# Order of the high and low products of the channel blocks, and the place of their low parts, in an encoder block in split precision

## The chip, the cores and the metric

The program runs on one core of a Trainium2 chip. The metric is the device time of one execution in microseconds. Before the change it is 1772.78 us, the median of three runs (1772.76 to 1772.98).

## The reference

The reference is one layer of a bidirectional encoder on 256 tokens and 2048 channels, in float32:

```
proj = x @ w_in                          # q, k, v, r, af, ab, hy_u, gate_logits
y_gla = gla(q, k, v, r, af, ab, ...)     # chunked gated linear attention, both directions
y_hy  = hyena(hy_u, ...)                 # gated long convolutions
mix = (g0 * (y_gla @ w_gla_o) + g1 * (y_hy @ w_hy_o)) @ w_out
h = layernorm(alpha * x + mix)
out = layernorm(alpha * h + square(relu(h @ w_ff1)) @ w_ff2)
```

q and k have 1024 columns each, w_ff1 has 8192.

## The kernel before, in words

Every weight arrives in float32 and is split into a high part (rounded to the type that TensorE multiplies at full rate) and a low part (what is left). ScalarE casts the high part, VectorE subtracts it from the source to give the low part. Activations are split in the same way and lie as `act[:, kt, 0 or 1, tokens]`: for each of 16 row tiles `kt`, 256 columns of high parts and then 256 of low parts. Three products are wanted for each pair of tiles: high by high, high by low, low by high.

There are two kinds of weight blocks, of 128 x 2048 numbers each, split in halves of 1024 columns. In a *token block* (r, v, g, u, the output projections) the activation tile is loaded into TensorE and the weights stream, 512 columns at a time. In a *channel block* (the gate ranks, q, k, and f, the first matrix of the MLP) the weight tile of 128 columns is loaded and the activation streams. The high tile meets 512 columns at once (high and low activations, a *wide* product), the low tile only the 256 high columns (a *narrow* product). A channel block has 16 tiles, so 16 wide and 16 narrow products, all summed into one bank of PSUM; the two halves of the bank are added afterwards.

`channel_products` (L187) issues one half of a channel block, eight tiles. The first half issues its eight wide products (L193) and then its eight narrow ones (L197); the second half the eight narrow ones and then the eight wide ones. A block is so 8 wide, 16 narrow, 8 wide.

It is called from three places. `channel_pair` (L215) does the blocks of q and k that the opening of the kernel has not already done: 4 of q and 8 of k. `ff1_first` (L1340) does the first eight blocks of f. Three of these are begun earlier, token half by token half, and ended in `finish_block` (L233), which calls `channel_products` for the second half of the third one only; the other five are plain. `ff_pairs` (L1418) does the remaining 56 blocks of f, one in each of its `SLOTS` steps, between the products of the second MLP matrix (called w, L1378 to L1380: all 512 columns wide, 21 in a step, 15 ahead of the block and 6 behind it).

`weight_half` (L151) hands out the tiles of a half: a high tile from three buffers in turn and a low tile from three others in turn. A low buffer has 1032 columns. With `by_channel` the low part takes columns 0 to 1023, without it columns 8 to 1031:

```
return (wp.tile([P, D // 2], F32R, tag="whi", bufs=3, name=f"whi{n}_{h}"),
        lo[:, 0:D // 2] if by_channel else lo[:, 8:])
```

`fetch` (L112) loads a block and splits it by way of `weight_half` and `split_hi_lo` (L103), some blocks ahead of its use; blocks 0 to 16 (gate ranks, q, k) and 177 to 184 (the first eight of f) are by channel. In `ff_pairs` the same is done by `half_split` (L1331), by channel as well.

The order of the instructions on each engine comes from a planner with its own costs; within `ff_pairs` the casts and subtractions are kept in program order.

Of the kernel before, what the change touches and what calls it, by code (L numbers as in the profile page):

```python
# [20 lines left out]
KT = D // P  # L21
# [9 lines left out]
W_OUT_END = 177  # L31
LEAD = 8
FF_PAIRS = W_OUT_END + LEAD
# [16 lines left out]
def block_kernel(  # L50
# [26 lines left out]
    MM = nc.tensor.matmul  # L77
# [19 lines left out]
    def psum_main(name):  # L97
        return mmp.tile([P, 512], F32, tag="mm", name=name)
# [4 lines left out]
    def split_hi_lo(hi, lo, src):  # L103
        return (nc.scalar.copy(hi, src),  # L104
                nc.vector.tensor_tensor(lo, src, hi.bitcast(F32), op=ALU.subtract))  # L105
# [6 lines left out]
    def fetch():  # L112
        n = fetched[0]
        if n >= stop_at[0]:
            return
        fetched[0] = n + 1
        raw = wp.tile([P, D], F32, tag="raw", bufs=3, name=f"raw{n}")
        nc.sync.dma_start(raw, wblk[n])
        parts = []
        for h in range(2):  # L120
            hi, lo = weight_half(n, h, n < 17 or W_OUT_END <= n < FF_PAIRS)
            last_low[0] = split_hi_lo(hi, lo, raw[:, h * 1024:(h + 1) * 1024])[1]
            parts.append((hi, lo))
            if paced[0]:
                tc.keep_in_program_order(last_low[0])
                fill()
        queue.append(parts)
# [10 lines left out]
    def fill(every=False):  # L138
        tick[0] += 1
        budget[0] = min(budget[0], PACE / 2) + PACE  # L140
        while filling:
            e = min(filling, key=lambda e: e[:2])
            if not every and (e[0] > tick[0] or e[2] > budget[0]):
                break
            filling.remove(e)
            budget[0] -= e[2]
            e[3]()
# [3 lines left out]
    def weight_half(n, h, by_channel=False):  # L151
        i = low_turn[0] % 3
        low_turn[0] += 1
        lo = (base, wp, wp)[i].tile([P, D // 2 + 8], F32R, tag=f"wlo{i}", bufs=1, name=f"wlo{n}_{h}")
        return (wp.tile([P, D // 2], F32R, tag="whi", bufs=3, name=f"whi{n}_{h}"),
                lo[:, 0:D // 2] if by_channel else lo[:, 8:])
# [21 lines left out]
    def next_block():  # L178
        fetch()
        return queue.popleft()  # L180

    FULL = slice(0, L)
# [1 line left out]
    def channel_psum(name):  # L184
        return psum_main(name).rearrange("p (a b) -> p a b", a=2)

    def channel_products(ps, act, half, kts, ts=FULL, opens=True):  # L187
        hi, lo = half
        at = [(kt, slice(kt % 8 * P, (kt % 8 + 1) * P)) for kt in kts]

        def high():
            for kt, js in at:
                MM(ps[:, :, ts], hi[:, js], act[:, kt, :, ts], start=(kt == 0 and opens), stop=(kt == KT - 1))  # L193

        def low():
            for kt, js in at:
                MM(ps[:, 0, ts], lo[:, js], act[:, kt, 0, ts], start=False, stop=False)  # L197

        for part in (high, low) if kts[0] == 0 else (low, high):
            part()  # L200
# [14 lines left out]
    def channel_pair(act, name, dst, scale=1.0):  # L215
        for c in range(2):
            ps = channel_psum(f"{name}_{c}")
            parts = next_block()
            for h in range(2):
                channel_products(ps, act, parts[h], range(8 * h, 8 * h + 8))  # L220
            channel_sum(dst[:, c], ps, f"{name}_l{c}", scale)
            pump()

    def high_by_tokens(ps, act, half, kts, ts):
        for kt in kts:
            MM(ps[:, :, ts], half[0][:, kt % 8 * P:(kt % 8 + 1) * P], act[:, kt, :, ts],
               start=(kt == 0 and ts.start == 0), stop=False)

    def low_of_all(ps, act, half, kts):
        for kt in kts:  # L230
            MM(ps[:, 0], half[1][:, kt % 8 * P:(kt % 8 + 1) * P], act[:, kt, 0], start=False, stop=(kt == KT - 1))

    def finish_block(ps, act, parts, n):  # L233
        for h in range(n):
            high_by_tokens(ps, act, parts[h], range(8 * h, 8 * h + 8), slice(P, L))
        for h in range(n):
            low_of_all(ps, act, parts[h], range(8 * h, 8 * h + 8))
        for h in range(n, 2):
            channel_products(ps, act, parts[h], range(8 * h, 8 * h + 8))

    def token_half(pss, act, half, tbs, kt0, ends=(0, KT - 1), order=lambda ins: ins):
        hi, lo = half
# [54 lines left out]
    with tc.tile_pool(name="xp", bufs=1) as xp, tc.tile_pool(name="xq", bufs=1) as xq:  # L297
# [44 lines left out]
        for k0, n in PIECES:  # L342
            raw = pieces[k0]
            kts = range(k0, k0 + n)
# [11 lines left out]
            if k0 == 0:  # L356
                hi, lo = places[0]
# [162 lines left out]
    for i in range(2 * NCH):  # L520
        c, o = divmod(i, 2)
        n = 4 + (i * 21) // 15
# [16 lines left out]
    for _ in range(2):  # L539
        fetch()  # L540
# [487 lines left out]
    def resident_pieces(parts, order=lambda ins: ins):  # L1028
        for part in parts:
            n = fetched[0]  # L1030
            fetched[0] = n + 1
            raw = wp.tile([P, D], F32, tag="raw", bufs=3, name=f"raw{n}")
            nc.sync.dma_start(raw, wblk[n])
            for h, (hi, lo) in enumerate(part):
                order(split_hi_lo(hi, lo, raw[:, h * 1024:(h + 1) * 1024])[1])
        return parts

    def resident(slots):
        return resident_pieces([[(hi[:, c:c + 1024], lo[:, c:c + 1024]) for c in (0, 1024)] for hi, lo in slots])

    def halves(pool, tag, name):
        t = pool.tile([P, 4, D], F32R, tag=tag, name=name)
        return [(t[:, 0], t[:, 1]), (t[:, 2], t[:, 3])]
# [71 lines left out]
    parts = resident([x0] + halves(ep, "f", "wr1"))  # L1115
# [5 lines left out]
    for tb in range(NT):  # L1121
        column_products(pss, mT, parts, [tb], 1)
        if tb == 1:
            fetch()
# [113 lines left out]
    def cast(hi, src):  # L1238
        return pin(nc.scalar.copy(hi, src))  # L1239

    def rest(lo, src, hi):
        return VT(lo, src, hi.bitcast(F32), ALU.subtract)
# [81 lines left out]
    def block_load(p):  # L1324
        if block_raw[p % 2] is None:
            block_raw[p % 2] = ep.tile([P, D], F32, tag=("xl", "fraw")[p % 2], name=f"fraw{p}")
        nc.sync.dma_start(block_raw[p % 2], wblk[FF_PAIRS + 1 + 2 * p])
# [1 line left out]
    half_parts = {}  # L1329

    def half_split(p, h):  # L1331
        hi, lo = weight_half(FF_PAIRS + 1 + 2 * p, h, True)
        src = block_raw[p % 2][:, h * 1024:(h + 1) * 1024]
        cast(hi, src)
        rest(lo, src, hi)
        half_parts[p, h] = (hi, lo)
        if h and p + 2 < SLOTS:
            block_load(p + 2)

    def ff1_first():  # L1340
        begun = begin_three()
        for c2 in range(LEAD // 2):
            for c in range(2):
                if begun:
                    ps, parts, n = begun.pop(0)
                    finish_block(ps, hT, parts, n)
                else:
                    ps = channel_psum(f"f{c2}_{c}")
                    parts = next_block()
                    for h in range(2):  # L1350
                        channel_products(ps, hT, parts[h], range(8 * h, 8 * h + 8))
                summed = quad_sum(c2, c, ps, f"f{c2}_l{c}")
                at = 2 * c2 + c
                if at in (LEAD - 4, LEAD - 3):
                    block_load(at - LEAD + 4)
                if at in (LEAD - 3, LEAD - 2):
                    ring_load(at - LEAD + 3)
                if at == LEAD - 2:
                    plain_split(0)
                    pair_split(0)  # L1360
            squares(c2)
            forms(c2)
            for g in ((), (0,), (1, 2), (3,))[c2]:
                zc = z1[:, 1, g * 512:(g + 1) * 512]
                with tc.issue_after(summed.ins):
                    nc.vector.tensor_tensor(zc, zc, rows1[:, 1, g * 512:(g + 1) * 512], op=ALU.add)
# [51 lines left out]
    def ff_pairs():  # L1418
        pss = [psum_side(f"w{j}") if j not in (2, 3, 4) else psum_main(f"w{j}") for j in range(7)]
        joins = []  # L1420
        for s in range(SLOTS):
# [12 lines left out]
            if more:  # L1434
                plain_split(s + 1)
                half_split(s + 1, 0)
# [9 lines left out]
            if more:  # L1446
                half_split(s + 1, 1)
# [40 lines left out]
    for h in range(2):  # L1488
        half_split(0, h)
# [30 lines left out]
    def quarters(*tiles):  # L1520
        at = [t[:, k:k + 1024] for t in tiles for k in range(0, t.shape[1], 1024)]
        return [[(at[0], at[1]), (at[2], at[3])], [(at[4], at[5]), (at[6], at[7])]]
# [4 lines left out]
    with tc.issue_after(last_low[0].ins):  # L1527
        parts = resident_pieces(quarters(*own, *spare), keep)
# [8 lines left out]
    parts = [half for block in parts for half in block]  # L1537
# [6 lines left out]
    ps = psum_main("w2_33_0")  # L1544
# [31 lines left out]
    for at, n in CENTRED[:3]:  # L1576
        po[at] = psum_side(f"lo{at}")
        parts = [(unit, z[:, at:at + 512]) for z in zg] if at < 1024 else [(ident, z1[:, 1, at:at + 512])]
# [169 lines left out]
```

## Time and profile before

| | |
|---|---|
| median of the runs | 1772.78 us |
| the profiled execution | 1773.26 us |
| its span | 1771.4 us |
| TensorE busy | 1763.8 us (100%), 8771 products |
| weight loads on TensorE | 1490.0 us (84%) |
| VectorE busy | 1460.9 us (82%) |
| ScalarE busy | 1048.4 us (59%) |
| GpSimd busy | 186.5 us (11%) |

The span is the stretch that the profile shows; the execution has 1.86 us more around it. PE is TensorE's products, PEld its weight loads, DVE VectorE, ACT ScalarE. Products are pipelined: one lasts 389 ns (wide) or some 280 ns (narrow) from start to end, but the next begins before it ends. What a product costs is the time from its start to the next start. A row of the timeline merges neighbours of one kind; its length runs to the end of the last of them.

### The profile page before, as it was taken

Reading aid. Unit: us, or ns where it says so; the run is one execution under the profiler, and the core shown is the slowest. Engines: PE = TensorE matmul, PEld = TensorE weight load, DVE = VectorE, ACT = ScalarE, POOL = GpSimd, SP = SyncE. Lnnn points to the kernel's source line nnn. Section 1 sums busy time; section 2 is a strip of 40 time slices with the busy share of each in tenths; the row PEclk is TensorE's granted clock in tenths of the full one; section 3 lists DMA queues with packets and bytes.
Section 4 is the critical chain, followed back from the end, with each engine's and each line's share of the span. In section 5 each row is a group of like instructions: output and inputs, shape, how many; then the busy total and the mean of one; then the engine's idle time right before and its main releaser. Section 6 shows DMA issues by size and latency. Waiting matters only on the chain.

```text
span 1771.4 us, 23597 instructions
## 1 busy us (share of the span) xinstructions
PE 1763.8 (100%) x8771; PEld 1490.0 (84%) x8771; DVE 1460.9 (82%) x1899; ACT 1048.4 (59%) x1446; POOL 186.5 (11%) x243
## 2 busy tenths in 40 slices
PE   9999999999999999999999999999999999999998
PEld 7888888888888888888888889888888888888886
DVE  6789996777688888888845558889999999999998
ACT  6587876787344444444444446666766666666653
POOL 1001111000110101021000000011111111111100
PEclk9999999999999999999999999999999999999999
DMA  8678888634796868797555664688878788888864
GB/s 329 230 252 265 290 258 257 199 141 173 262 299 222 279 232 273 232 287 256 192 192 187 264 247 165 207 267 253 258 242 277 241 251 256 269 249 247 267 207 168
DMA packets 87299, 427.13 MB, mean 241 GB/s; under 512 B 9800, under 2 KB 14296, under 8 KB 45584
## 3 DMA queue, kind: packets, MB, share of 16 engines
q1 hardware_dynamic: 47664, 336.35, 51.5%
q0 software_dynamic: 30560, 67.38, 18.3%
q10 hardware_dynamic: 8960, 21.89, 3.5%
q8 instruction: 69, 1.13, 0.3%
q14 instruction: 46, 0.38, 0.1%
HBM read 382.12 MB, written 12.06 MB: 223 GB/s over the span
## 4 chain that ended last, share of the span: by engine, by line
PE 96%; DVE 3%; issue 1%; ACT 0%; DVEq 0%
PE f L193 13%; PE f L197 6%; PE w L1379 5%; PE w L1380 5%; PE w L1378 5%; PE g L251 3%; PE g L252 3%; PE ux L251 3%; PE ux L252 3%; PE g L250 3%; PE ux L250 3%; PE k L193 2%; PE r L251 2%; PE r L252 2%; PE v L251 2%; PE v L252 2%
## 5 line engine op out<-in xcount | busy, mean ns | idle before, releaser
L104 ACT CAST whi<-raw 128x1024 fp32r<-128x1024 f32 x360 | 377.8, 1054 | 401.0 <-PE ux L252 86.7
L105 DVE TENSOR_TENSOR wlo<-raw,whi 128x1024 fp32r<-128x1024 f32 x360 | 438.2, 1222 | 158.1 <-ACT whi L104 154.2
L193 PE MATMUL f<-hT,whi 128*128 128x512 f32 x984 | 244.3, 391 | 0.0
L193 PEld LDWEIGHTS f<-hT,whi 128*128 128x128 f32 x984 | 180.2, 188 | 35.0
L1236 DVE TENSOR_TENSOR wlo<-fraw,whi 128x1024 fp32r<-128x1024 f32 x112 | 136.9, 1223 | 13.5 <-ACT whi L1239 9.8
L197 PEld LDWEIGHTS f<-hT,wlo 128*128 128x128 f32 x984 | 123.8, 188 | 5.2
L1239 ACT CAST whi<-ring 128x1024 fp32r<-128x1024 f32 x56 | 59.0, 1054 | 113.9 <-DVE ring L1236 113.9
L1299 POOL DMA_DIRECT2D ring<-wblk x56 | 48.6, 868 | 726.3 <-DVE ring L1236 719.9
L197 PE MATMUL f<-hT,wlo 128*128 128x256 f32 x984 | 124.9, 279 | 0.0
L1239 ACT CAST whi<-fraw 128x1024 fp32r<-128x1024 f32 x112 | 117.6, 1050 | 0.0
L1239 ACT CAST b_h<-ring 128x1024 fp32r<-128x1024 f32 x112 | 87.9, 834 | 22.3 <-PE w L1380 21.6
L251 PE MATMUL g<-wlo,xT 128*128 128x512 f32 x256 | 100.1, 391 | 0.0
L251 PE MATMUL ux<-wlo,xT 128*128 128x512 f32 x256 | 99.9, 390 | 0.0
L252 PE MATMUL ux<-whi,xT 128*128 128x512 f32 x256 | 99.9, 390 | 0.0
L252 PE MATMUL g<-whi,xT 128*128 128x512 f32 x256 | 99.8, 390 | 0.0
L250 PE MATMUL g<-whi,xT 128*128 128x512 f32 x256 | 92.2, 390 | 0.0
L250 PE MATMUL ux<-whi,xT 128*128 128x512 f32 x256 | 89.2, 389 | 0.0
L1236 DVE TENSOR_TENSOR ring<-ring 128x512 f32<-128x512 f32 x112 | 77.2, 689 | 1.9
L1236 DVE TENSOR_TENSOR b_l<-ring,b_h 128x1024 fp32r<-128x1024 f32 x56 | 68.4, 1222 | 8.1 <-ACT b_h L1239 8.0
L1236 DVE TENSOR_TENSOR wlo<-ring,whi 128x1024 fp32r<-128x1024 f32 x56 | 68.6, 1225 | 2.1 <-ACT whi L1239 0.3
L1236 DVE TENSOR_TENSOR fa<-ring,fa 128x1024 fp32r<-128x1024 f32 x56 | 68.3, 1220 | 0.0
L1300 POOL DMA_DIRECT2D ring<-ring x56 | 67.2, 1201 | 0.0
(529 smaller groups left out, 4257.8 us busy)
## 6 DMA issues: line engine op xcount, KB each, us to landing
raw<-wblk SPq DMA_DIRECT2D x188, 1024.0 KB, 5.1
fraw<-wblk SPq DMA_DIRECT2D x56, 1024.0 KB, 4.9
ring<-wblk SPq DMA_DIRECT2D x56, 1024.0 KB, 7.0
ring<-wblk POOLq DMA_DIRECT2D x56, 256.0 KB, 4.4
ring<-ring POOLq DMA_DIRECT2D x56, 256.0 KB, 5.2
conv_sb<-conv_rows SPq DMA_DIRECT2D x12, 1024.0 KB, 8.7
w<-w4s ACTq DMA_DIRECT2D x16, 512.0 KB, 5.1
Td<-T POOLq DMA_DIRECT2D x32, 256.0 KB, 5.3
```

The costliest lines, as they stand in the source:

```text
L104: return (nc.scalar.copy(hi, src), nc.vector.tensor_tensor(lo, src, hi.bitcast(F32), op=ALU.subtract))
L105: nc.vector.tensor_tensor(lo, src, hi.bitcast(F32), op=ALU.subtract))
L193: MM(ps[:, :, ts], hi[:, js], act[:, kt, :, ts], start=(kt == 0 and opens), stop=(kt == KT - 1))
L197: MM(ps[:, 0, ts], lo[:, js], act[:, kt, 0, ts], start=False, stop=False)
L250: order(MM(pss[tb], sh, wh, start=(kt == ends[0]), stop=False))
L251: order(MM(pss[tb], sh, wl, start=False, stop=False))
L252: order(MM(pss[tb], sl, wh, start=False, stop=(kt == ends[1])))
L1236: return pin(nc.vector.tensor_tensor(dst, a, b, op=op))
L1239: return pin(nc.scalar.copy(hi, src))
L1378: pin(MM(ps, sh, wh, start=(p == begin), stop=False))
L1379: MM(ps, sh, wl, start=False, stop=False)
L1380: pin(MM(ps, sl, wh, start=False, stop=(p == end - 1)))
```

## The change

```diff
@@ fetch
-            hi, lo = weight_half(n, h, n < 17 or W_OUT_END <= n < FF_PAIRS)
+            hi, lo = weight_half(n, h, n == W_OUT_END)
@@
-    def channel_products(ps, act, half, kts, ts=FULL, opens=True):
+    def channel_products(ps, act, half, kts, ts=FULL, opens=True, grouped=False):
         hi, lo = half
         at = [(kt, slice(kt % 8 * P, (kt % 8 + 1) * P)) for kt in kts]
+        if not grouped:
+            for kt, js in at:
+                MM(ps[:, :, ts], hi[:, js], act[:, kt, :, ts], start=(kt == 0 and opens), stop=False)
+                MM(ps[:, 0, ts], lo[:, js], act[:, kt, 0, ts], start=False, stop=(kt == KT - 1))
+            return
@@ finish_block
-            channel_products(ps, act, parts[h], range(8 * h, 8 * h + 8))
+            channel_products(ps, act, parts[h], range(8 * h, 8 * h + 8), grouped=True)
@@ half_split
-        hi, lo = weight_half(FF_PAIRS + 1 + 2 * p, h, True)
+        hi, lo = weight_half(FF_PAIRS + 1 + 2 * p, h)
```

Each tile of a plain channel block now has its wide and its narrow product one behind the other, 16 times in a block, in the order of the tiles. The low parts of these blocks start at column 8 of their buffers, where those of the token blocks start. The half that `finish_block` ends keeps its order, and block 177 (`W_OUT_END`), which is begun by token halves, and the halves that the opening and `begin_three` split themselves keep their low parts at column 0. No product, cast, subtraction or transfer is added or removed.

## Rows read from the trace of the kernel before

**Rows 1.** Page, part 1: busy time, share of the span, instructions.
```profile
PE 1763.8 (100%) x8771; PEld 1490.0 (84%) x8771; DVE 1460.9 (82%) x1899; ACT 1048.4 (59%) x1446; POOL 186.5 (11%) x243
```
**Rows 2.** Page, part 4: the chain of waits, by engine.
```profile
PE 96%; DVE 3%; issue 1%; ACT 0%; DVEq 0%
```
**Rows 3.** Windows: PE, PEld, DVE, ACT, POOL busy; clock, DMA share, GB/s.
```profile
33.00:105.00 72.00, 72.00 (x413) 62.66 (x412) 52.17 (x78) 47.70 (x75) 5.01 (x9) 1.00 0.70 244
1111.00:1143.00 32.00, 32.00 (x181) 27.96 (x180) 26.30 (x40) 21.09 (x33) 1.80 (x2) 1.00 0.65 218
1306.90:1317.20 10.30, 10.30 (x55) 8.83 (x54) 9.43 (x11) 7.69 (x11) 1.75 (x2) 1.00 0.83 261
1143.00:1718.00 575.00, 574.73 (x2963) 492.10 (x2962) 531.60 (x673) 384.93 (x508) 96.61 (x110) 1.00 0.82 252
```
**Rows 4.** Tiles f, q, k: count, duration min/median/max in ns, first and last start.
```profile
L193 PE MATMUL f<-hT,whi x984: 389/389/400, 1110.8 to 1713.3; 128*128 128x512 f32 x197
...
L193 PE MATMUL q<-xT,whi x64: 387/389/496, 32.5 to 55.1; 128*128 128x512 f32 x64
...
L193 PE MATMUL k<-xT,whi x128: 387/389/403, 55.3 to 104.9; 128*128 128x512 f32 x128
```
**Rows 5.** Timeline of PE, five neighbouring blocks of f: start, length, count.
```profile
1114.43 2.03 PE L197 MATMUL f<-hT,wlo 128*128 128x256 f32 x16
1116.29 3.82 PE L193 MATMUL f<-hT,whi 128*128 128x512 f32 x16
...
1131.01 2.03 PE L197 MATMUL f<-hT,wlo 128*128 128x256 f32 x16
...
1136.54 2.03 PE L197 MATMUL f<-hT,wlo 128*128 128x256 f32 x16
```
**Rows 6.** Timeline of PE, one step of `ff_pairs`.
```profile
1302.11 0.39 PE L1378 MATMUL w<-fa,fa 128*128 128x512 f32 x1
...
1306.87 1.98 PE L193 MATMUL f<-hT,whi 128*128 128x512 f32 x8
1308.69 2.03 PE L197 MATMUL f<-hT,wlo 128*128 128x256 f32 x16
1310.55 2.00 PE L193 MATMUL f<-hT,whi 128*128 128x512 f32 x8
1312.39 0.39 PE L1378 MATMUL w<-fa,fa 128*128 128x512 f32 x1
...
1317.15 1.98 PE L193 MATMUL f<-hT,whi 128*128 128x512 f32 x8
```
**Rows 7.** Timeline of PE, end of the opening.
```profile
30.40 0.40 PE L337 MATMUL open<-xT,open_k 128*128 128x512 f32 x1
30.64 0.40 PE L337 MATMUL open<-xT,open_sp 128*128 128x512 f32 x1
30.87 0.39 PE L339 MATMUL open<-xT,open_sp 128*128 128x256 f32 x2
31.10 0.40 PE L337 MATMUL open<-xT,open_k 128*128 128x512 f32 x1
...
31.80 0.40 PE L337 MATMUL open<-xT,open_k 128*128 128x512 f32 x1
...
32.49 1.31 PE L193 MATMUL q<-xT,whi 128*128 128x512 f32 x5
```
**Rows 8.** Timeline of PE around a single narrow product among wide ones.
```profile
47.94 0.28 PE L425 MATMUL mlp<-gx,mlp_ws 128*128 128x256 f32 x1
48.05 2.70 PE L193 MATMUL q<-xT,whi 128*128 128x512 f32 x11
```
**Rows 9.** Timeline of PE, a run of narrow products in the opening.
```profile
25.06 1.12 PE L339 MATMUL open<-xT,open_G 128*128 128x256 f32 x8
26.02 0.63 PE L337 MATMUL open<-xT,open_k 128*128 128x512 f32 x2
```
**Rows 10.** Timeline of DVE: subtractions that give low parts of f.
```profile
1126.57 1.22 DVE L105 TENSOR_TENSOR wlo<-raw,whi 128x1024 fp32r<-128x1024 f32 x1
...
1311.02 1.22 DVE L1236 TENSOR_TENSOR wlo<-fraw,whi 128x1024 fp32r<-128x1024 f32 x1
...
1314.68 1.23 DVE L1236 TENSOR_TENSOR wlo<-fraw,whi 128x1024 fp32r<-128x1024 f32 x1 [0.52 <-ACT whi L1239]
```
**Rows 11.** Timeline of ACT: a cast into the high buffer freed by the block.
```profile
1311.19 1.05 ACT L1239 CAST whi<-ring 128x1024 fp32r<-128x1024 f32 x1 [2.18 <-DVE ring L1236]
```

## The prediction

> **What bounds the kernel now.** I read the busy times first, then the chain of waits, then windows over the stretches that the change touches, then single starts in the timeline. TensorE is busy for the whole span [rows 1], and the chain that ends last is 96% TensorE [rows 2]. In the stretches with the channel blocks (33 to 105 us for q and k, 1111 to 1143 us for the first of f, 1143 to 1718 us for the rest) it is busy to within 0.3 us, at a granted clock of 1.00, that is at the upper of its two levels [rows 3]. Nothing that another engine does there is on the path: the time is the sum of the distances between product starts. So the change is worth what it does to these distances, unless it makes TensorE wait.
>
> **How many products move.** f has 984 wide products in `channel_products`, of which 8 belong to the half that keeps its order, so 976; q has 64 and k 128 [rows 4]. That is 1168 pairs of a wide and a narrow product, 73 blocks of 16 pairs: 56 in `ff_pairs`, 5 in `ff1_first`, 12 of q and k.
>
> **What a pair costs now.** Four neighbouring blocks take from 1114.43 to 1136.54 us, 5.528 us each, or 345.5 ns for a pair [rows 5]. In a step of `ff_pairs` the same shows in parts: 8 wide in 1.82 us, 16 narrow in 1.86 us (116 ns each), 8 wide in 1.84 us (230 ns each) [rows 6].
>
> What is the least that a pair can take? The 21 products of w between 1302.11 and 1306.87 us, all wide, take 226.7 ns each [rows 6]. Half of that, 113.3 ns, is my estimate for a narrow one; a pair would take 340.0 ns. The run order so loses 87 ns a block: about 27 ns in the 8 wide products behind the narrow run, about 50 ns in the narrow run, and the rest where wide turns to narrow. A narrow run on other tiles, in the opening, takes 0.96 us for 8, 120 ns each [rows 9]; so the loss changes with the tiles.
>
> **What a pair will cost.** No stretch of the trace has wide and narrow strictly in turn. Three rows come near:
> - At the end of the opening two wide and two narrow products take turns. From 30.40 to 32.49 us there are three rounds, six pairs in 2.09 us: 348.3 ns a pair [rows 7]. The first round has 0.47 us for its two wide products (235 ns each instead of 226.7), then 0.23 us for its two narrow ones.
> - A single narrow product between wide ones takes 0.11 us, and the 10 distances behind it (11 products in 2.70 us, less the last one's 0.39) average 231 ns; the surplus over 226.7 is 43 ns, for one narrow product [rows 8]. The kernel of the change gives each wide product only one distance in which to pay. With 235 ns for the wide one [rows 7] and 116 for the narrow one [rows 6] a pair has 351 ns; I take this as the upper end.
> - The lower end is 340.0 ns, nothing lost at all.
>
> What speaks for a loss is that a wide product just behind a narrow one is slow in every case that the trace has: 230 ns over eight of them [rows 6], 235 [rows 7], 231 over ten [rows 8]. In turn, every wide product stands behind a narrow one. I take 348.3 ns, since rows 7 is the nearest to the new order: as many loads for as much streaming, and the same mix.
>
> The Trainium skill (TensorE: Matmul & The Clock Gate, section "Step-by-step: what each phase is for") says that weights and streamed columns come through two separate read ports, so that loading the next tile takes no bandwidth from the running product. By that rule wide products would all be alike, the order would cost nothing, and a pair would take 340.0 ns. The trace does not agree: products of the same 512 columns, at the same clock, take 226.7 ns in one place and 230 to 235 in another [rows 6, 7].
>
> **The sum.** A block of 16 pairs at 348.3 ns takes 5573 ns, 45 more than now. In `ff_pairs` the block now ends with a narrow product, and the wide products of w behind it pay too: behind the last narrow product of the opening five wide ones take 1.31 us, 0.92 us for four distances once the last one's 0.39 is taken off, 13 ns over 4 x 226.7 [rows 7]; after a long narrow run it is 27 ns (1.84 us less 8 x 226.7) [rows 6]. I take 13. So 56 blocks x 58 ns = 3.2 us and 17 blocks x 45 ns = 0.8 us, together 4.0 us. The profiled execution of 1773.26 us (span 1771.4 and 1.86 around it) would become 1777.3; it is 0.48 us above the median of the runs, so the forecast is 1772.78 + 4.0 = 1776.8 us. With 351 ns and 27 ns it would be 56 x 115 + 17 x 88 ns = 7.9 us, 1780.7 us.
>
> **What I cost at nothing.** *Low parts needed earlier.* In the first half of a block the first narrow product comes 0.23 us behind the first wide one instead of 1.82. The tightest case that I found in f has its low part written by 1127.79 us (start 1126.57 and 1.22) for the narrow products at 1131.01, 3.2 us ahead [rows 5, 10]; it keeps 1.6. In `ff_pairs` the low part is written by 1312.24 for the block that starts at 1317.15 [rows 6, 10]. If that cover were gone, TensorE would wait up to 1.6 us in a block. *High parts of the second half* are needed about 1 us earlier, but the low parts behind them, split later and needed as early as before, have been the late ones. *Buffers freed later.* The first half's high tile is let go 0.9 us later (1309.6 us instead of 1308.69); the cast into such a buffer starts at 1311.19 and waits for VectorE [rows 11]. The second half's low tile is let go with the end of the block (1312.4 instead of 1310.55); the next subtraction into it starts at 1314.68 [rows 10]. VectorE has 9.43 us of work in a step of 10.3 us [rows 3], which stays. *DMAs* are issued as before, none moved past another on a queue. *The planner* may put the filter products elsewhere among the blocks of k: I allow 0.5 us either way.
>
> **Rivals.**
> - *A, in step.* Wide and narrow in turn may settle in a rhythm without loss, as the wide products of w do (226.7 ns, 21 in a row [rows 6]); with the low parts at the new place the load under each wide product may cost nothing. For it: long rows of one kind do settle, and the narrow run at the present place costs 116 ns where another costs 120 [rows 6, 9], so the place counts. Against it: rows 7 and 8, where narrow products stand among wide ones and cost is shown each time. A pair takes 340.0 ns: 73 x 87 ns = 6.4 us less, and 56 x 13 ns back for the wide products of w, 5.6 us: 1767.2 us (1766.4 if w pays nothing). It decides from a mean pair below 345.5 ns.
> - *B, it cancels.* The wide product pays 230 to 233 ns and the narrow one 113.3 to 115, since no narrow product stands behind another: 343.3 to 348 ns, on the middle what it is now. 1771 to 1775.5 us, likeliest 1773.3. For it: only in a run does each narrow product wait for the load of another; against it: rows 7 has its narrow products in twos and no wide one at 230.
> - *C, low parts late.* The planner issues the subtractions of a channel block in another order and TensorE waits for low parts in the blocks of q, k and the first of f: 17 blocks x 0.3 us = 5 us over the forecast, 1781.9 us. Against it: the spare 1.6 us.
>
> **How the numbers follow.** My forecast (348 ns, 1774.5 to 1780.7 us) has 0.44, A 0.28, B 0.25, C 0.03. What a measurement of this kernel can tell from no change is about 0.2%, 3.5 us. A is faster by more than that, but for 0.01; B stays within it but for 0.02; the forecast's lower part, 0.10, lies within it too, the rest of it and C are slower. Faster 0.27, same 0.34, slower 0.39. The range has to reach to A, since leaving it out leaves out more than 2 in 10: 1766.2 to 1780.4 us; the forecast's own is 1774.5 to 1780.7.
>
> **What would show it.** In the timeline of the changed kernel, single products of f by turns: wide starts 0.348 us apart on the mean show the forecast, 0.340 shows A, 0.345 B. The span of a step of `ff_pairs`, now 10.28 us (1306.87 to 1317.15), would become 10.34; with A it is 10.20 to 10.21. Products of w behind a block a few ns apart more than 226.7 show the payment at its end. Any idle time of TensorE ahead of f, q or k that ends with VectorE shows C. The forecast is wrong if the mean pair is under 345.5 ns.

## The result, and the profile after

The changed kernel takes 1782.97 us, the median of six runs (1781.87 to 1783.74), beside 1772.75 us before in the same runs (1772.60 to 1772.98). The ratio is 1.0057, with an interval of 1.0044 to 1.007: slower by 10.2 us. The forecast was 1776.8 us, its range ended at 1780.4; the side was right, the size too small.

The profiled execution of the changed kernel is the fastest of the six, 1781.87 us (span 1780.1), so its rows account for 8.7 us more than the span of before. The medians lie further apart because this execution is 1.1 us below its median and the profiled one of before 0.5 us above its own. Where the other executions spend that time, no trace shows.

The page has first the busy times, then the chain by engine. They answer to [rows 1, 2]:

```profile
PE 1771.4 (100%) x8771; PEld 1491.0 (84%) x8771; DVE 1460.7 (82%) x1899; ACT 1050.5 (59%) x1446; POOL 186.8 (10%) x243
...
PE 95%; DVE 4%; ACT 1%; issue 1%; DVEq 0%
```

The same number of products keeps TensorE busy for 7.6 us longer. The other engines have the same numbers of instructions; ScalarE is busy 2.1 us longer, VectorE 0.2 us less. The chain is TensorE's as before. The waits of PE, whole execution (waiting line, what it waited for, us in total, times, longest):

```profile
PE warm L318 <- DVE ones_sb L380: 1.5, 1, 1.5
PE g L256 <- DVE wlo L105: 1.0, 1, 1.0
PE w L255 <- DVE zr L1241: 0.8, 1, 0.8
```

No wait stands ahead of a product of f, q or k. The one of 1.0 us is new: a token block of g waits for a low part. Yet ux, the next matrix but one, begins only 0.27 us later than before (451.67 against 451.40). The sums of the distances between starts show why. The opening takes 0.7 us less and the products of q and k themselves 0.7 us more. Behind them the products of g, v and z take 1.5 us more, the wait among it, and those of uv, s and yt 1.2 us less; the planner has put them in another order. That q and k end 1.38 us later (106.46 against 105.08) is for the most part 12 products of X (1.4 us) that are now done among them. From the first product of f to the first of the last token block (lo) it is 676.98 us instead of 668.52, 8.46 more. So what the trace shows lies in f.

The stretch of `ff_pairs` by windows (columns as in [rows 3]) and one step of it by the timeline of PE (start, length; what counts is the distance to the next start):

```profile
1143.00:1726.00 583.00, 582.22 (x2961) 493.43 (x2960) 532.65 (x675) 386.58 (x508) 96.78 (x110) 1.00 0.81 248
```
```profile
1310.05 0.39 PE L192 MATMUL f<-hT,whi 128*128 128x512 f32 x1
1310.28 0.28 PE L193 MATMUL f<-hT,wlo 128*128 128x256 f32 x1
1310.39 0.40 PE L192 MATMUL f<-hT,whi 128*128 128x512 f32 x1
1310.62 0.28 PE L193 MATMUL f<-hT,wlo 128*128 128x256 f32 x1
1310.74 0.40 PE L192 MATMUL f<-hT,whi 128*128 128x512 f32 x1
1310.98 0.28 PE L193 MATMUL f<-hT,wlo 128*128 128x256 f32 x1
1311.10 0.40 PE L192 MATMUL f<-hT,whi 128*128 128x512 f32 x1
...
1315.58 0.28 PE L193 MATMUL f<-hT,wlo 128*128 128x256 f32 x1
1315.69 0.40 PE L1383 MATMUL w<-fa,fa 128*128 128x512 f32 x1
1315.92 0.40 PE L1384 MATMUL w<-fa 128*128 128x512 f32 x1
1316.16 0.39 PE L1385 MATMUL w<-fa,fa 128*128 128x512 f32 x1
...
1320.48 0.39 PE L192 MATMUL f<-hT,whi 128*128 128x512 f32 x1
```

The first pair takes 0.34 us, the other fifteen 5.30 us (1310.39 to 1315.69), 353.3 ns each. By the single starts, the median over 56 blocks, three pairs make a round: wide 233, 241, 236 and narrow 117, 120, 113 ns. No distance is a wait; five of the six are longer than the 226.7 or 113.3 of an undisturbed product. A block takes 5640 ns instead of 5527, the products of w behind it 27 ns more than undisturbed, where before they paid nothing. A step takes 10.43 us instead of the 10.28 of [rows 6].

### The profile page after: what moved, and what is told of

Same layout as the page of the kernel before. It is cut to its first block, busy times and chain, and to the rows that moved or that the text cites. A ratio compares the mean times of both kernels' runs of the same rounds, so it can differ in the third digit from the quotient of the medians.

```text
span 1780.1 us, 23595 instructions
## 1 busy us (share of the span) xinstructions
PE 1771.4 (100%) x8771; PEld 1491.0 (84%) x8771; DVE 1460.7 (82%) x1899; ACT 1050.5 (59%) x1446; POOL 186.8 (10%) x243
## 4 chain that ended last, share of the span: by engine, by line
PE 95%; DVE 4%; ACT 1%; issue 1%; DVEq 0%
PE f L192 13%; PE f L193 6%; PE w L1383 5%; PE w L1384 5%; PE w L1385 5%; PE ux L256 3%; PE ux L257 3%; PE ux L255 3%; PE g L256 3%; PE g L257 3%; PE g L255 3%; PE k L192 2%; PE r L256 2%; PE r L257 2%; PE ho L257 2%; PE uv L257 2%
## 5 line engine op out<-in xcount | busy, mean ns | idle before, releaser
L192 PE MATMUL f<-hT,whi 128*128 128x512 f32 x976 | 346.9, 398 | 0.0
L193 PE MATMUL f<-hT,wlo 128*128 128x256 f32 x976 | 273.9, 281 | 0.0
L193 PEld LDWEIGHTS f<-hT,wlo 128*128 128x128 f32 x976 | 184.3, 189 | 2.2
```

## One measure for all kernels

In the table is the median step of `ff_pairs` for each kernel that ran, worked out from the starts of its trace: 16 wide and 16 narrow products of f and 21 wide ones of w. Undisturbed that is 37 x 226.67 + 16 x 113.33 = 10,200 ns. The loss over it comes in whole multiples of 6.67 ns (16 cycles of the clock's upper level, 2.4 GHz; the granted clock was 1.00 in every trace); n counts them. "Behind" is what w pays behind the block, "column" where the low parts of channel blocks begin in their buffers (4 bytes to a column). The ratio is to the kernel before in shared runs; e8 was executed once and has none.

| kernel | order, column | block, ns | behind | step, ns | n | median us | ratio (interval) |
|---|---|---|---|---|---|---|---|
| before | runs, 0 | 5527 | 0 | 10287 | 13 | 1772.75 | |
| after | turn, 8 | 5640 | 27 | 10427 | 34 | 1782.97 | 1.0057 (1.0044 to 1.007) |
| e1 | turn, 0 | 5646 | 41 | 10447 | 37 | 1783.80 | 1.0062 (1.0047 to 1.0077) |
| e2 | runs, 8 | 5567 | 0 | 10327 | 19 | 1775.22 | 1.0013 (1.0004 to 1.0023) |
| e3 | turn, 8, in `ff_pairs` alone | 5640 | 27 | 10427 | 34 | 1781.15 | 1.0047 (1.0032 to 1.0062) |
| e4 | twos, 8 | 5563 | 10 | 10333 | 20 | 1776.84 | 1.0023 (1.0013 to 1.0033) |
| e5 | 2 twos, then turn, 8 | 5543 | 10 | 10313 | 17 | 1775.30 | 1.0015 (1.0006 to 1.0025) |
| e6 | runs, 4 | 5527 | 0 | 10287 | 13 | 1772.45 | 0.9999 (0.9989 to 1.0008) |
| e7 | runs, 0, all 32 bytes on | 5527 | 0 | 10287 | 13 | 1772.52 | 0.9999 (0.999 to 1.0008) |
| e8 | turn, 8, all wide | 7253 | 0 | 12013 | 0 | 1898.04 | |
| e9 | runs, 2 | 5540 | 0 | 10300 | 15 | 1773.59 | 1.0005 (0.9995 to 1.0014) |
| e10 | runs, 6 | 5547 | 0 | 10307 | 16 | 1773.89 | 1.0008 (0.9998 to 1.0017) |
| e11 | turn, 4 | 5537 | 10 | 10307 | 16 | 1774.52 | 1.0009 (1.0 to 1.0019) |
| e12 | turn, 2 | 5557 | 63 | 10380 | 27 | 1779.13 | 1.0036 (1.0022 to 1.0049) |
| e13 | turn, 6 | 5646 | 27 | 10433 | 35 | 1782.41 | 1.0055 (1.004 to 1.007) |
| e14 | turn, 8, hT 16 bytes on | 5560 | 47 | 10367 | 25 | 1778.46 | 1.0032 (1.0019 to 1.0045) |
| e15 | twos, 4 | 5557 | 10 | 10327 | 19 | 1775.80 | 1.0018 (1.0008 to 1.0027) |
| e16 | 2 twos, then turn, 6 | 5644 | 16 | 10420 | 33 | 1781.82 | 1.0053 (1.004 to 1.0066) |
| e17 | 1 two, then turn, 6 | 5639 | 28 | 10427 | 34 | 1781.97 | 1.0052 (1.0038 to 1.0066) |
| e18 | 3 turns, 1 two, turn, 6, in `ff_pairs` alone | 5497 | 10 | 10267 | 10 | 1772.09 | 0.9997 (0.9988 to 1.0006) |

## Experiments

**The order or the place?** The change has two parts, so each is done alone (e1, e2), and both in `ff_pairs` alone (e3).

e1, on the kernel after, puts the low parts back:

```diff
-            hi, lo = weight_half(n, h, n == W_OUT_END)
+            hi, lo = weight_half(n, h, n < 17 or W_OUT_END <= n < FF_PAIRS)
-        hi, lo = weight_half(FF_PAIRS + 1 + 2 * p, h)
+        hi, lo = weight_half(FF_PAIRS + 1 + 2 * p, h, True)
```

> The order alone: wide and narrow products in turn as in the change, the low parts left at column 0. Theory of rhythm (the distance of a product depends on the order of wide and narrow and on the place of the tile that is loaded beneath it; after the change the wide ones of f lie 233, 241, 236 ns apart in rounds of three and the narrow ones 117, 120, 113, 353.3 ns a pair, where the runs had 345.5): in turn no wide product is free of a narrow neighbour here either, so 348 to 356 ns a pair and 1776 to 1785 us. Rival, the place alone (the low parts at column 8 cost, the order nothing): 1772.8 us within 1. Rival, the planner (order of the other engines' work and low parts that come late): a step of ff_pairs of 10.28 us as before, and idle time of TensorE ahead of f, q or k.

e2 makes the opposite edit on the kernel before: runs, column 8.

> The place alone: runs as before, the low parts at column 8. Theory of rhythm: the narrow runs go to 120 ns a product, as the run of the opening on other tiles (16 narrow 1.91 us instead of 1.86), the last wide product before them saves the 8 ns that it loses now: a block 5.57 us instead of 5.53, 73 x 0.04 = 2.9 us more, 1775.7 us (1774.5 to 1777). Rival, the place alone: as the changed kernel, 1782 to 1784 us. Rival, the planner: anything between, with idle time of TensorE.

e3 on the kernel after: the flag of `fetch` as before, and

```diff
@@ channel_pair, ff1_first
-                channel_products(ps, act, parts[h], range(8 * h, 8 * h + 8))
+                channel_products(ps, act, parts[h], range(8 * h, 8 * h + 8), grouped=True)
```

> In turn and at column 8 in ff_pairs alone; the blocks of q, k and the first of f in runs, with their low parts at column 0. Theory of rhythm: 56 steps x 140 ns (113 in the block, 27 in the wide products of w behind it) = 7.8 us, 1780.6 us, and nothing before 1140 us. Rival, the planner in the blocks of q, k and the attention behind them: 1772.8 us plus at most 2.

The order alone costs 11.0 us, the place alone 2.4 us, both together 10.2: they don't add up. With runs at column 8 the block of e2 shows where its 40 ns go (timeline of PE):

```profile
1307.13 1.98 PE L193 MATMUL f<-hT,whi 128*128 128x512 f32 x8
1308.94 2.08 PE L197 MATMUL f<-hT,wlo 128*128 128x256 f32 x16
1310.85 2.00 PE L193 MATMUL f<-hT,whi 128*128 128x512 f32 x8
```

16 narrow products take 1.91 us instead of the 1.86 of [rows 6], 120 ns each; the eight wide ones ahead take 1.81 instead of 1.82, those behind are as before. e3 has 8.3 us of the loss (beside 1772.83 in shared runs), as 56 steps by 140 ns (7.8 us) ask: the loss is in the repeated step, not in waits that q and k might bring.

**The forecast's own price: twos.** The forecast took the price of a pair from products by twos [rows 7]. e4 puts that order into the kernel, e5 uses it only to enter the turn, both on the kernel after:

```diff
-            for kt, js in at:
-                MM(... hi[:, js] ...)
-                MM(... lo[:, js] ...)
+            for i in range(0, 8, 2):                  # e4
+            groups = ([at[0:2], at[2:4]] if kts[0] == 0 else []) + [[e] for e in at[4 if kts[0] == 0 else 0:]]  # e5
+                for kt, js in (the group): MM(... hi[:, js] ...)
+                for kt, js in (the group): MM(... lo[:, js] ...)
```

> The changed kernel with the products by twos: two wide, then the two narrow of the same tiles, at column 8. Theory of rhythm: the rhythm of the end of the opening, 348.3 ns a pair, 5573 ns a block and 10 to 27 ns in w behind it: 56 x 55 to 72 + 17 x 45 ns = 3.9 to 4.8 us, 1776.7 to 1777.6 us, the time that was forecast for the change. Rival, the place alone, and rival, a fixed price for each turn from wide to narrow and back (353.3 - 340 = 13.3 ns for each pair of turns): the first 1782 to 1784 us; the second half the turns, 8 x 13.3 = 107 ns a block over 5440, 5546, and so 1774.1 us.

> The changed kernel, but the first four tiles of a block by twos (two wide, two narrow), and only the other twelve in turn. Theory of rhythm (there are several rhythms of the same order, and the one that holds is the one entered): in the changed kernel the first blocks of q, which follow the opening's twos, run in turn at 232, 118, 231, 112, 233, 117, 231, 113 ns, 346.7 ns a pair, while those entered from wide products alone run at 353.3. So here 1384 ns for the four tiles and 12 x 346.7 = 4160, 5544 ns a block, 13 in w behind it: 56 x 30 + 17 x 17 ns = 2.0 us, 1774.8 us (1774 to 1776). Rival, a fixed price of the order: 1384 + 12 x 353.3 = 5624 ns a block, 27 behind it: 56 x 124 + 17 x 97 = 8.6 us, 1781.4 us.

Twos take 5563 ns a block, 347.7 a pair, and w pays 10 behind: the forecast's 348.3 and 13 were good prices for twos. They were no prices for the turn. And in e5 the same turn, at the same column, is cheap when it comes in from two rounds of twos:

```profile
1390.74 0.63 PE L194 MATMUL f<-hT,whi 128*128 128x512 f32 x2
1391.21 0.39 PE L196 MATMUL f<-hT,wlo 128*128 128x256 f32 x2
1391.44 0.40 PE L194 MATMUL f<-hT,whi 128*128 128x512 f32 x1
1391.67 0.28 PE L196 MATMUL f<-hT,wlo 128*128 128x256 f32 x1
...
1392.13 0.40 PE L194 MATMUL f<-hT,whi 128*128 128x512 f32 x1
```

The rows show the second round of twos and the first pair behind it. From 1391.44 to 1392.13 two pairs take 0.69 us, and so on to the block's end: wide 232 and 231, narrow 118 and 113, 346.7 ns a pair instead of 353.3. A fixed price for each pair of the turn is refuted. Two rounds of twos are no sure way in either: in a block of k of the same run (from 60.90 us) they led into 353.3 ns.

**Without narrow products.** e8, on the kernel after, streams all 512 columns past the low tile too:

```diff
-                MM(ps[:, 0, ts], lo[:, js], act[:, kt, 0, ts], ...)
+                MM(ps[:, :, ts], lo[:, js], act[:, kt, :, ts], ...)
```

> The changed kernel with the low tile's product widened to all 512 columns (it adds the low-by-low product, which the others leave out): the same loads of high and low tiles in turn, at column 8, but no narrow product. Theory of rhythm: without a narrow product nothing is lost, 2 x 226.7 = 453.4 ns a pair as in w, 7254 ns a block instead of 5640, and no payment behind the block: 56 x 1587 + 17 x 1614 ns = 116.3 us over the changed kernel, 1899 us. Rival, the place or the turn of high and low tiles itself costs: 8 to 13 ns a pair stay, 1168 of them, 1909 to 1915 us.

```profile
1400.00 0.39 PE L192 MATMUL f<-hT,whi 128*128 128x512 f32 x1
1400.23 0.39 PE L193 MATMUL f<-hT,wlo 128*128 128x512 f32 x1
1400.45 0.39 PE L192 MATMUL f<-hT,whi 128*128 128x512 f32 x1
```

A pair takes 0.45 us; a block takes 7253 ns, 32 x 226.7, n = 0. The same tiles, loaded in the same order from the same places, lose nothing. So it isn't the changing of tiles; the loss takes narrow products. It does not take two lengths beside each other: in a run of their own the narrow ones lose too (120 ns each in e2). Whether a narrow product is simply too short for the load of the next tile wasn't tried.

**The place, in runs.** e6, e9 and e10 move the low parts of the kernel before; e7 moves everything:

```diff
-                lo[:, 0:D // 2] if by_channel else lo[:, 8:])
+                lo[:, 4:4 + D // 2] if by_channel else lo[:, 8:])   # e6; e9: 2, e10: 6
+    base.tile([P, 8], F32, tag="shift", name="shift")               # e7 alone, ahead of the first tile
```

> The kernel before with the low parts of the channel blocks at column 4 instead of 0, the runs as they are. Theory of rhythm, with a place that counts by degrees: narrow products somewhere between the 113.3 ns of a first one and the 120 of column 8, a block of 5.47 to 5.58 us, 1768.5 to 1776 us. Rival, two classes of place (like the other operands or not): column 4 is not like them and gives what column 0 gives, 116.6 ns a narrow product, 1772.8 us within 0.7.

> The kernel before with one unused tile of 32 bytes in front, so that every tile lies 32 bytes further on and the distances between them stay. Theory of rhythm, by places relative to each other: nothing changes, 1772.8 us within 0.7. Rival, absolute place: the wide products' 226.7 ns themselves are a price of the place; at 2.4 GHz 512 columns take 213.3 ns by count, so up to 13 ns for each of some 7000 wide products could go (down to 1680 us) or as much come.

> The kernel before with its low parts at column 2 (8 bytes on), runs kept. At columns 0 and 4 a block of f took 5527 ns, at column 8 5567. If the price of the place goes by steps of 32 bytes, column 2 is as column 0: 5527 ns, 1772.5 to 1772.8 us. If it is graded with the distance, or has a best place in between, the narrow run takes other times: any narrow mean under 116 ns (16 of them, 73 blocks) gives up to 73 x 16 x 3 ns = 3.5 us, 1769 us, a version faster than both.

> As before with low parts at column 6 (24 bytes on). Steps of 32 bytes: 5527 ns a block, 1772.5 to 1772.8 us. Graded: half way between columns 4 and 8, 5547 ns, 1772.6 + 73 x 0.020 = 1774.1 us.

Columns 0, 2, 4, 6 and 8 have n = 13, 15, 13, 16 and 19. Neither steps of 32 bytes (nor two classes of place) nor a graded price fit: column 2 would have to be as column 0, or column 4 dearer than column 2. That column 6 took just the 5547 ns that the graded price asked for was luck. All tiles together may move by 32 bytes without a change (e7), while the low parts alone, moved by as much, cost 6 steps (n = 19 instead of 13). So their own place doesn't decide alone. Everything moved by less than 32 bytes wasn't run.

**The place, in turn.** Up to here I held that the turn is dear at any place, since columns 0 and 8 were alike. e11 was meant to confirm it: e1 with the low parts at column 4.

> The kernel after, each high and low product in turn, but with the low parts of channel blocks at column 4 (the flags as before). If the turn's loss comes from the order at any place, a block takes 5640 to 5646 ns as at columns 8 and 0, 1783 to 1784 us. If the place can free the turn from its loss (rival A of the prediction, for another place), 5440 to 5560 ns a block, 1768 to 1776 us.

It refuted it: 1774.52 us. The timeline of a block's beginning, behind the wide products of w, as in the kernel after:

```profile
1390.19 0.39 PE L192 MATMUL f<-hT,whi 128*128 128x512 f32 x1
1390.41 0.28 PE L193 MATMUL f<-hT,wlo 128*128 128x256 f32 x1
1390.53 0.39 PE L192 MATMUL f<-hT,whi 128*128 128x512 f32 x1
...
1391.22 0.40 PE L192 MATMUL f<-hT,whi 128*128 128x512 f32 x1
```

Here two pairs take 0.69 us from 1390.53 to 1391.22, 346.6 ns each (229 and 234, 117.5 and 112). Of the 140 ns that the turn costs a step, 120 are gone by a move of 16 bytes. Then columns 2 and 6, and in e14 the kernel after with the activations of f moved in place of the low parts:

```diff
-    hT = act_tile(ep, "hT", "hT")
+    hT = ep.tile([P, KT * 2 * L + 8], F32R, tag="hT", name="hT")[:, 4:4 + KT * 2 * L].rearrange(
+        "p (k a l) -> p k a l", a=2, l=L)
```

> High and low product in turn, low parts of channel blocks at column 2 (8 bytes on). At columns 0 and 8 a pair of f took 353 ns once it had come in from wide products, at column 4 346.6. If the odd places (not on a 32-byte step) all keep the turn in the cheap rhythm: 5537 to 5550 ns a block, 1774 to 1775 us. If only the half step of 16 bytes does: about 5640 ns, 1782 to 1784 us.

> As the last, low parts at column 6 (24 bytes on). Odd places alike: 5537 to 5550 ns a block, 1774 to 1775 us. Only 16 bytes: about 5640 ns, 1782 to 1784 us.

> The kernel after, low parts at column 8, but the activations of f (hT) moved 16 bytes on instead, in a tile 8 columns longer. If what counts is where the loaded tile lies against the streamed one, f falls into the cheap rhythm (5537 ns a block, 61 x 0.11 us less: about 1776 us; q and k stay dear). If it is the place itself, or where the low tile lies against the high one, f stays at 5640 ns and the time at 1782 to 1784 us.

In turn, columns 0, 2, 4, 6 and 8 have n = 37, 27, 16, 35 and 34. By the steady pairs there are two groups: columns 2 and 4 settle at 346.7 ns, columns 0, 6 and 8 at 353.3, so neither alternative of e12 and e13 came true. The large n of column 2 is the 63 ns that w pays behind the block. In e14 n falls from 34 to 25 in f, while blocks of k, whose activations did not move, take up to 5661 ns, the same as in the kernel after. So the place of the streamed tile counts as well as that of the loaded ones. If only the distance from the low tile to hT counted, e14 would be a copy of e11; it isn't, its steady pair is 225 and 122 ns. Whether the distances decide, of which tiles, or each tile's own place below 32 bytes, isn't told apart.

e15, the twos of e4 at column 4, tells whether another order gains from the place too:

> Two wide and two narrow in turn, low parts at column 4. At column 8 the twos took 5563 ns a block (1776.8 us). If the place helps them as it helped the turn (about 110 ns a block): 5455 ns, 73 x 0.11 us less, 1769 us, faster than both kernels. If the twos were in the cheap rhythm already, 5530 to 5565 ns, 1774.5 to 1777 us.

Hardly: n = 19 instead of 20. The place that suits the turn is of no use to the twos.

**The way in.** In e13 the first two blocks of q lost nothing at all (timeline of PE; the opening ends at 31.87), while a block of k in the same run took some 353 ns a pair:

```profile
31.64 0.39 PE L344 MATMUL open<-xT,open_sp 128*128 128x256 f32 x2
31.87 0.39 PE L192 MATMUL q<-xT,whi 128*128 128x512 f32 x1
32.10 0.27 PE L193 MATMUL q<-xT,wlo 128*128 128x256 f32 x1
...
32.55 0.39 PE L192 MATMUL q<-xT,whi 128*128 128x512 f32 x1
...
60.81 0.40 PE L192 MATMUL k<-xT,whi 128*128 128x512 f32 x1
61.05 0.28 PE L193 MATMUL k<-xT,wlo 128*128 128x256 f32 x1
...
61.52 0.40 PE L192 MATMUL k<-xT,whi 128*128 128x512 f32 x1
```

Two pairs of q start 0.68 us apart (32.55 less 31.87), 340 each; the two of k 0.71. The rhythm without loss of rival A exists. e16 (e5 at column 6) and e17 (the same with `[at[0:2]]` and `at[2 ...]`, one round of twos) try to reach it:

> The first four tiles of a block by twos, the twelve others in turn, low parts at column 6. With the turn at column 6 the first two blocks of q, which come behind the opening's twos, took 228 and 112 ns in turn, 340.0 a pair, nothing lost (5440 ns a block), while all others took 353. If the way in decides the rhythm and the place only which rhythms there are: four tiles by twos 1384 ns as at column 8, then 12 x 340 = 4080, together 5464 ns, 63 less than before; 56 of these, 10 ns paid by w behind each, and 17 x 63 in the other blocks, less what the filter products between them spoil: 3 to 4.5 us faster than before, 1768 to 1769.5 us. If the 340 hung on something else in those two blocks (the activations of q and k, the opening's own tiles): 5540 to 5650 ns a block, 1774 to 1783 us.

> The same with only the first two tiles by twos, so that the turn begins one round earlier. If any narrow product next to a narrow one lets the turn in without loss: 14 x 340 + 690 = 5450 ns, 1768 to 1769 us. If the round matters: 5540 to 5650 ns, 1774 to 1783 us.

Both failed in `ff_pairs`. But in e17 single blocks had it. One of them, and the next block, which lost it again:

```profile
1119.50 0.40 PE L194 MATMUL f<-hT,whi 128*128 128x512 f32 x1
...
1120.20 0.63 PE L194 MATMUL f<-hT,whi 128*128 128x512 f32 x2
1120.67 0.40 PE L196 MATMUL f<-hT,wlo 128*128 128x256 f32 x2
1120.91 0.39 PE L194 MATMUL f<-hT,whi 128*128 128x512 f32 x1
1121.14 0.27 PE L196 MATMUL f<-hT,wlo 128*128 128x256 f32 x1
1121.25 0.39 PE L194 MATMUL f<-hT,whi 128*128 128x512 f32 x1
...
1125.33 0.39 PE L194 MATMUL f<-hT,whi 128*128 128x512 f32 x1
...
1125.67 0.62 PE L194 MATMUL f<-hT,whi 128*128 128x512 f32 x2
1126.13 0.40 PE L196 MATMUL f<-hT,wlo 128*128 128x256 f32 x2
1126.37 0.40 PE L194 MATMUL f<-hT,whi 128*128 128x512 f32 x1
...
1126.72 0.40 PE L194 MATMUL f<-hT,whi 128*128 128x512 f32 x1
```

Twos (the rows with x2) behind a dear round, 0.70 us for two pairs from 1119.50 to 1120.20, led into 0.34 us a pair (1120.91 to 1121.25). Twos behind lossless pairs (0.34 us, 1125.33 to 1125.67) led out of it: 0.35 from 1126.37 on, and 0.353 on the mean. e18 builds that way in on purpose, in `ff_pairs` alone, on the kernel before:

```diff
+        if turn:
+            lead = 3 if kts[0] == 0 else 8
+            for group in [[e] for e in at[:lead]] + [at[lead:lead + 2]] + [[e] for e in at[lead + 2:]]:
+                for kt, js in group: MM(... hi[:, js] ...)
+                for kt, js in group: MM(... lo[:, js] ...)
+            return
-        hi, lo = weight_half(FF_PAIRS + 1 + 2 * p, h, True)
+        hi, lo = weight_half(FF_PAIRS + 1 + 2 * p, h, col=6)
```

> The kernel before, but the blocks of f in the repeated steps have their low parts at column 6 and this order: three tiles in turn, two by twos, eleven in turn; all other blocks stay in runs at column 0. In the last run each of the five pairs of twos that stood behind a round of 236, 120, 233, 118 took about 241, 231, 117, 118 and let the turn in at 227 and 113; none behind another phase did. From the wide products of w the turn at column 6 went 235, 118, 228, 117, 233, 118, 236, 120. So by the theory that the way in picks the rhythm: 235, 118, 228, 117, 233, 118, then 241, 231, 117, 118, then 11 x 340: 5496 ns a block, 31 less than before, 56 x 31 = 1.7 us, less up to 13 ns for w behind each: 1771.0 to 1771.8 us beside 1772.6. If the rhythm can't be foreseen from the phase: 5600 to 5650 ns a block, 1777 to 1780 us.

```profile
1306.08 0.40 PE L195 MATMUL f<-hT,whi 128*128 128x512 f32 x1
...
1307.13 0.63 PE L195 MATMUL f<-hT,whi 128*128 128x512 f32 x2
1307.60 0.40 PE L197 MATMUL f<-hT,wlo 128*128 128x256 f32 x2
1307.84 0.39 PE L195 MATMUL f<-hT,whi 128*128 128x512 f32 x1
...
1311.24 0.39 PE L195 MATMUL f<-hT,whi 128*128 128x512 f32 x1
1311.46 0.27 PE L197 MATMUL f<-hT,wlo 128*128 128x256 f32 x1
1311.58 0.40 PE L1387 MATMUL w<-fa,fa 128*128 128x512 f32 x1
```

Eleven pairs take 3.74 us (1307.84 to 1311.58), 340 each, in all 56 blocks; the distances by single starts are those expected (235, 118, 228, 117, 233, 118, 241, 231, 117, 118, then 227 and 113). The block takes 5497 ns (5496 expected), the step has n = 10 beside 13. The median is 1772.09 us beside 1772.65 in shared runs, 0.6 less where 0.8 to 1.6 were expected. The interval of the ratio, 0.9988 to 1.0006, holds 1, so the kernel is not shown to be faster; the shorter step is shown by the trace. No kernel here beats the one before by a measured time.

## Why the prediction was wrong in its size

- **What bounds the kernel** was right. TensorE has no wait ahead of f, q or k, and the difference in the trace is the sum of distances between its starts.
- **That the order costs** was right in sign and kind: wide products lose where narrow ones stand among them (e8: nothing lost without narrow ones). It is no law of the order, though: e18's turn loses nothing.
- **The step that failed** is "I take 348.3 ns, since rows 7 is the nearest to the new order", and with it the upper end of 351 ns and the 13 ns behind the block. A pair took 353.3 ns and w paid 27: 113 + 27 = 140 ns a step in place of 45 + 13 = 58. 56 steps at 140 ns are 7.8 us, the forecast had 3.2; five blocks of `ff1_first` add 0.6, and these 8.4 are the 8.46 seen between f and lo. The 348.3 ns were measured well, for twos (347.7 in e4); they were carried over to singles as if a mix had one price.
- **What stood in its place:** a pair has no price of its own. The same order took 340.0, 346.7 or 353.3 ns a pair with the place of its tiles (e11 against e1 and after) and with what stood ahead of it (e5 against after; e18). The opening's rows showed one such rhythm of several. The bound of 351 was a sum of two single distances taken from two different rhythms, so it bounded nothing. In its four blocks of q, the first of which comes in from the opening's twos, the kernel after did take 346.7 ns, close to the forecast; in f it comes in from the wide products of w.
- **The place** had no price in the sum at all. Alone it costs 2.4 us (e2), and at column 4 the change would have cost 1.7 us beside before instead of 10.2 (e11: 1774.52 against 1772.80 in shared runs; it leaves the rest as in the kernel after).
- **Rival A** (340 ns) was wrong for this kernel, though the rhythm is real (e13, e18). The Trainium skill (TensorE: Matmul & The Clock Gate, section "Step-by-step: what each phase is for") lets loads and streamed columns go through ports of their own, by which, as the prediction worked out, all wide products would be alike. They aren't: 226.7 ns in w and in e8, 233 to 241 in the changed kernel's turn, at a granted clock of 1.00. Whether loads and streams meet there, or something else slows the products, no run shows.
- **Rival B** (it cancels) was wrong on both products: the narrow ones took 116.7 ns on the mean, where it had 113.3 to 115, the wide ones 236.7, where it had 230 to 233. Its times (1771 to 1775.5 us) do not quite follow from its prices either: 343.3 to 348 ns a pair give 1770.2 to 1775.7 us, or 1770.9 to 1776.4 with 13 ns paid by w in each step.
- **Rival C** (low parts late) did not occur: no wait ahead of f, q or k. The margins of 1.6 us held, and what was costed at nothing cost nothing in f. A late low part did stop TensorE once, for 1.0 us, but in a token block of g, which C had not named. The planner's allowance of 0.5 us held as well: with all gains and losses 0.27 us were left at ux. Of the 0.5 us that the sum had for q and k (their own products took 0.7 us more) no more than that reached f.

## What to carry to other kernels

When TensorE never waits, read the distance between starts, not the length of a product, and compare it with that of a long row of one kind: the difference is what the order and the place cost. A price per pair read from one mix holds for that mix, its place and what stands ahead of it; for another order the honest range takes in all the rhythms that the trace shows, and a few more. Before an order is judged, try it with its tiles a few bytes on: here 16 bytes decided 9 of 11 us (e1 against e11).

## What the hardware showed that I had not expected

- The loss comes in steps of 6.67 ns: in the traces of all kernels the step of `ff_pairs` is 10,200 ns and a whole number of them, from 10 to 37 (0 over its own 12,013 in e8).
- The rhythm is stable and reproducible. All 56 blocks of a kernel take the same time to 1 ns, e18's distances could be told in advance from e13 and e17, and one round of twos can switch between rhythms (e17, e18).
- The places of the loaded tiles and of the streamed one count in units below 32 bytes (columns 2, 4 and 6 differ, and so does e14), and an order that is dear in one place is cheap in another.
- A steady turn had only three prices in all these kernels: 340.0, 346.7 or 353.3 ns a pair, that is no, one or two steps of 6.67 ns.
- Why it is so, what delays the products, no run here shows.
